# A second level of Strassen for two of the seven products of seven SwiGLU pairs

## The chip, the cores and the metric

The kernel runs on one core of a Trainium2 chip. The metric is the device time of one execution in microseconds (us). Three runs of the kernel before took 2426.53, 2428.89 and 2431.48 us; their median, 2428.89 us, is the time before.

## The reference, cut to what matters

One layer of a hybrid decoder for a prompt of 1024 tokens and eight single sample tokens that use the same weights. Three token mixers (a gated convolution, a state-space scan, attention into a memory) are merged by `w_merge_o`; then comes the part that is changed:

```python
xp = xp + swiglu(rmsnorm(xp, norm_ffn_w[l]), w_ffn_gate[l], w_ffn_up[l], w_ffn_down[l])
...
y_prompt = rmsnorm(xp, norm_final_w)
```

The same is done for the samples. In words: with x the normalized activations (1024 features), h = silu(x·Wgate) * (x·Wup), and the output adds h·Wdown. FFN_HIDDEN is 2816, so Wgate and Wup are 1024 x 2816 and Wdown is 2816 x 1024. All is fp32.

## The kernel before, in words

**Layout.** Prompt and samples stand side by side as the 1032 columns (TT) of feature-major tiles of 128 partitions; half of them is HT = 516. A hidden block is 128 of the 2816 hidden features (22 blocks). A fp32 matrix product is done as three fp32r matmuls, hi·hi, hi·lo and lo·hi: every weight tile and every activation tile exists as `hi` (a copy in fp32r, on ScalarE) and `lo` (what the copy lost, a subtraction on VectorE). This pair of operations is called a split here: `st_split` (L251, its copy L254 and subtraction L255) for weights of 512 or 1024 columns, `split_to` (L392, L393 and L395) for activations.

**One level of Strassen.** Gate, up and most of down are done in pairs of hidden blocks (for down: pairs of output blocks) by `strassen` (L318). The activations are cut in four quadrants, features 0 to 511 and 512 to 1023 by columns 0 to 515 and 516 to 1031; the weights of the two blocks in four as well. Instead of eight quadrant products there are seven, each of a sum of weight quadrants with a sum of activation quadrants. The seven sums of activations are called forms, B11, T1, nT2, B21, T3, B22 and T4; they are made once (`form`, `last_forms`) and stay in SBUF as hi and lo tiles, six in the pool "acts" and T4 in the pool "fx". The sums of weights are made anew for every pair on VectorE: L293 and L294 in `st_sums`, L299 and L300 in `st_adds2`, all of 512 columns. `st_raw` loads the weights of a block. A product (`st_prod`, the matmul is L267) is 4 blocks of 128 features x 3 hi/lo combinations x 2 column pieces (256 and 260) = 24 matmuls, collected in a PSUM tile of 516 columns. PSUM tiles m0, m1 and m2 are used in turn; T3 is added to the tile that already holds nT2 (and B11), after VectorE or ScalarE have read it, T4 to the same one after T3. In an early chain L372 is VectorE's read of nT2, for which T3 waits, and L381 its read of T3, for which T4 waits.

**The pairs.** The loop at L1978 runs over eleven pairs of hidden blocks: (0,9), (1,5), (2,6), (3,7), (4,8), (11,15), (12,16), (13,17), (14,18), (10,19), (20,21). For each, `hidden_pair` (L1950) does a chain of products for gate (names g0, g1, ...) and one for up (u0, u1, ...; the number is that of the pair's first block). The first four pairs are called early: products B11 and B21 of their first block were made ahead by `st_early` (L271) and stored, so their chains have five products. The other seven pairs, numbered 4 to 10, have seven products for gate and seven for up. Behind gate and up follow silu, the product of both, four sums that make the forms of the down projection, and their stores to DRAM (`hf_d`; for the last pairs and (0,9) the plain blocks go to `h_d`).

**Down.** Two parts. In each, first the product of a single hidden block (or two) with its rows of Wdown, 16 groups of 6 (or 12) matmuls called pd (L2078, read from PSUM at L2083 to L2085); beside them the forms of the part are loaded and split (`hidden_forms`), and the weights of the first down pair are prepared (`st_begin`, L306). Then come four chains of seven products, `d00` to `d06` in part 0 and `d10` to `d16` in part 1 (in the trace with an m behind the name: d00m).

**What sets the order.** The engines run their queues in program order, and a scheduler in the framework orders the instructions by its own estimate of their durations when the program is built; `in_turn` fixes the order of loads and of splits among themselves, `tc.issue_after` puts an instruction behind another, and `tick` runs one piece of deferred work from the list `pend` at a marked place. Nearly all DMAs are issued by SyncE's one queue (SP), in order. GpSimd has work only in the scan, around 1000 to 1300 us of the span (L1040 scales the states, L1089 decays them). In that stage L168 and L178 are splits of weights and of activations, L1031 masks a product of 128 columns that it reads from PSUM, and L1059 multiplies 512 columns that it reads from PSUM.

Pools that are touched: "weights" with three raw, three hi and three lo tiles of 1024 columns, "acts" with 12 hi and 12 lo tiles, "ev" with five, "fx" with two, PSUM "sm" with two tiles.

Of the kernel before, what the change touches and what calls it, by code (L numbers as in the profile page):

```python
# [9 lines left out]
F32 = mybir.dt.float32  # L10
# [7 lines left out]
P = 128  # L18
D = 1024
T = 1024  # L20
# [23 lines left out]
def tile_kernel(ctx: ExitStack, tc, a, o):  # L44
# [9 lines left out]
    cp = ctx.enter_context(tc.tile_pool(name="const", bufs=1))  # L54
    wp = ctx.enter_context(tc.tile_pool(name="weights", bufs=3))
# [34 lines left out]
    tri = cp.tile([P, P], F32, tag="tri", name="tri")  # L90
# [140 lines left out]
    count = [0]  # L231

# [3 lines left out]
    HALF = ((0, 256), (256, HT))  # L236

# [50 lines left out]

    def st_sums(src1, src2, nm, sums, behind=None):
        raw1, raw2 = st_raw(src1, f"{nm}r1"), st_raw(src2, f"{nm}r2")  # L290
        sa = sums(f"{nm}sa")
        with nullcontext() if behind is None else tc.issue_after(behind):
            V.tensor_add(sa[:, :512], raw2[:, :512], raw2[:, 512:])  # L293
        V.tensor_add(sa[:, 512:], sa[:, :512], raw1[:, :512])  # L294
        return raw1, raw2, sa, st_split(sa, f"{nm}S")

    def st_adds2(raw1, raw2, sa, nm, sums):
        sb = sums(f"{nm}sb")
        V.tensor_add(sb[:, :512], raw1[:, :512], raw2[:, :512])  # L299
# [17 lines left out]
    def strassen(src1, src2, forms, nm, sums, outs, early=None, after_t3=None, ready=None, hook=None, add=False, begun=None, mid=None):  # L317
# [6 lines left out]
        tags = ("m0", "m1", "m2") if count[0] % 2 == 0 else ("m2", "m1", "m0")  # L324
# [87 lines left out]
    e_d = dram("e_d", [7, P, TT])  # L412
    q_d = dram("q_d", [8, P, TT])
# [8 lines left out]
    tail_sc = cp.tile([P, 1, 10, 8], F32, tag="tail_sc", name="tail_sc")  # L422
    tail_xc = cp.tile([P, 3, 11, 8], F32, tag="tail_xc", name="tail_xc")
    qs = cp.tile([P, 8, NS], F32, tag="qs", name="qs")
# [1135 lines left out]
    if True:  # L1560
# [212 lines left out]
        att_stack.close()  # L1773
        ph2 = ctx.enter_context(tc.tile_pool(name="ph2", bufs=1))
# [73 lines left out]
    def form_second(kt):  # L1848
        form("B21", kt, normed(kt + 4, 0))
# [57 lines left out]
    fx["T4"] = lambda part, nm: pfx.tile([P, 2, HT], F32R, tag=part, name=nm)  # L1907
# [36 lines left out]
    def last_forms():  # L1944
        for kt in range(4):
            t2, b21 = x2[kt][:, HS[0]], x2[kt + 4][:, HS[0]]
            V.scalar_tensor_tensor(t2, t2, -1.0, b21, op0=ALU.mult, op1=ALU.subtract)
            form("T4", kt, t2, freed[0])
# [29 lines left out]
    for n, (j, j2) in enumerate(pairs):  # L1978
# [18 lines left out]
        for f, t in enumerate((b11, t1, t2, b21, t3_, b22, t4)):  # L1997
            SY.dma_start(hf_d[f, n - 1], t)
# [58 lines left out]
    for part, js in enumerate(([0], [9, 10])):  # L2057
# [6 lines left out]
        begun = st_begin(*down_src(part, 0), f"d{part}0", ev_sums)  # L2064
# [3 lines left out]
        for m in range(KD):  # L2068
            if not part:
                x2[m] = big(f"x3_{m}")  # L2070
            for half in range(2):
# [12 lines left out]
                else:  # L2084
                    puts.append(S.copy(t, hv(ps)).ins)  # L2085
        count[0] += 1
# [180 lines left out]
```

## Time and profile before

| | |
|---|---|
| runs of the kernel before | 2426.53, 2428.89, 2431.48 us |
| profiled execution, in all | 2428.33 us |
| its span (first to last instruction) | 2426.6 us |
| mean granted TensorE clock | 0.998 |
| gate and up of pairs 4 to 10 | 1898 to 2178 us of the span |
| first part's pd products | 2178 to 2191 us |
| d00 | 2191 to 2212 us |
| DRAM traffic by DMA | 407.94 MB |

The span is the time between the first and the last instruction that the profiler recorded; the profiled execution's own time has 1.73 us more, which lie before and behind it. PE is the TensorE's matmul, PEld its weight load, DVE VectorE, ACT ScalarE, POOL GpSimd, SP SyncE, whose queue issues DMAs. In a row of the timeline or of the chain of waits the first number is the start in us from the span's beginning, the second the duration, then engine, line, operation, output tile and inputs with their sizes; in brackets stands the idle time before it and what ended it. In the chain, a row with "x120" is a run of so many instructions of one kind. In a row of groups the numbers behind the bar are busy time in all and mean duration in ns, then the idle time before the group's instructions. A row by stretches has start and end, length, and then for each engine the busy time with its count of instructions.

### The profile page before, as it was taken

The numbers are of one execution on the slowest core, as the hardware profiler recorded it, in microseconds if no ns is written. First come the engines' busy times: TensorE is split into PE (matmuls) and PEld (weight loads), VectorE is DVE, ScalarE is ACT, GpSimd is POOL, SyncE is SP. The second block draws the span as 40 slices with busy tenths as digits, with TensorE's granted clock in tenths as the row PEclk, the third lists the DMA queues.
The fourth block names the chain that finished last, engine by engine and source line by source line (L and its number), as shares of the span: only waits on it lengthen the run. The fifth ranks groups of instructions, "written<-read, shape, count | busy, mean of one in ns | idle before, by whom it ended". The sixth has DMA issues, their size and how long they took to land. (4 is left out here: it accounts for less than half of the span.)

```text
span 2426.6 us, 45180 instructions
## 1 busy us (share of the span) xinstructions
PE 2397.0 (99%) x18716; PEld 2279.9 (94%) x18716; DVE 1613.8 (67%) x2597; ACT 1091.9 (45%) x1740; POOL 106.9 (4%) x163
## 2 busy tenths in 40 slices
PE   8999999999999999999999999999999999999998
PEld 6999999999999999888888887899999999999998
DVE  6844677777777675568687773454777655567965
ACT  6643555455453543656555542223543333343423
POOL 0000000000000000212212000000000000000000
PEclk9999999999999999999999999999999999999999
DMA  6444423444354345768887797864455333354622
GB/s 203 136 150 164 135 84 114 140 140 131 112 158 118 106 126 179 225 223 272 257 283 215 252 337 234 276 213 150 148 178 168 101 104 103 94 178 154 192 88 79
DMA packets 357716, 407.94 MB, mean 168 GB/s; under 512 B 16270, under 2 KB 277502, under 8 KB 357503
## 3 DMA queue, kind: packets, MB, share of 16 engines
q1 hardware_dynamic: 334374, 341.79, 45.2%
q10 hardware_dynamic: 23137, 63.26, 6.8%
q8 instruction: 147, 2.41, 0.4%
q14 instruction: 58, 0.48, 0.1%
HBM read 288.85 MB, written 116.38 MB: 167 GB/s over the span
## 5 line engine op out<-in xcount | busy, mean ns | idle before, releaser
L1007 ACT ACTIVATE r<-r,acum 128x128 f32<-128x128 f32 x256 | 79.3, 391 | 3.5 <-DMA r<-ac_d 2.6
L796 DVE SCALAR_TENSOR_TENSOR ax<-u,prm,ax 128x1024 f32<-128x1024 f32 x44 | 56.4, 1282 | 0.0
L948 ACT ACTIVATE st<-st,es 128x128 f32<-128x128 f32 x128 | 41.3, 392 | 19.1 <-DMA st<-in_state_ssm_dram 14.5
L1040 POOL TENSOR_TENSOR xdd<-xdt,decst 128x512 f32<-128x512 f32 x32 | 34.3, 1072 | 284.2 <-DVE xdt L1036 278.4
L1034 DVE TENSOR_TENSOR r<-r,cbm 128x1024 f32<-128x1024 f32 x32 | 39.2, 1224 | 4.3 <-ACT r L1009 2.4
L950 DVE SCALAR_TENSOR_TENSOR st<-sr,dts,st 128x128 f32<-128x128 f32 x128 | 41.0, 355 | 0.4
L1059 DVE TENSOR_TENSOR y<-po,ea 128x512 f32<-128x512 f32 x28 | 19.3, 690 | 31.3 <-PE po L1055 31.3
L1076 PE MATMUL pss<-xdd,bT 128*128 128x512 f32 x64 | 34.5, 620 | 3.7 <-ACT bT L1033 3.1
L954 DVE SCALAR_TENSOR_TENSOR sr<-st,sr 128x128 f32<-128x128 f32 x128 | 36.1, 292 | 1.1
L1497 DVE TENSOR_TENSOR yr<-po,yr 128x1032 f32<-128x1032 f32 x8 | 9.8, 1230 | 39.5 <-PE po L218 39.5
L1063 PE MATMUL py<-r,xdt 128*64 128x128 f32 x512 | 35.0, 279 | 0.0
L1009 ACT ACTIVATE r<-r 128x1024 f32<-128x1024 f32 x32 | 33.9, 1058 | 0.7
L1089 POOL TENSOR_TENSOR s<-s,cdec 128x512 f32<-128x512 f32 x28 | 33.1, 1181 | 1.8 <-DVE s L1082 1.5
L1883 DVE TENSOR_TENSOR x<-pm,xT 128x516 f32<-128x516 f32 x15 | 10.4, 694 | 32.3 <-PE pm L1869 32.3
L1800 DVE TENSOR_TENSOR gt<-po,gt 128x1032 f32<-128x1032 f32 x8 | 9.9, 1232 | 32.4 <-PE po L218 31.1
L1063 PEld LDWEIGHTS py<-r,xdt 128*64 128x64 f32 x512 | 27.3, 136 | 4.4 <-issue 1.0
L1055 PE MATMUL po<-bc,s 128*128 128x128 f32 x224 | 29.6, 275 | 0.0
L1055 PEld LDWEIGHTS po<-bc,s 128*128 128x128 f32 x224 | 28.0, 191 | 1.0
L1612 ACT ACTIVATE pr<-psa,mx 128x256 f32<-128x256 f32 x32 | 14.9, 470 | 30.1 <-DVE mx L1610 30.1
L799 DVE SCALAR_TENSOR_TENSOR ax<-u,prm,ax 128x1032 f32<-128x1032 f32 x22 | 28.4, 1290 | 0.0
L1600 DVE SCALAR_TENSOR_TENSOR kc<-kc,qb 128x256 f32<-128x256 f32 x64 | 23.9, 423 | 6.3 <-DMA qb<-qs_d 6.3
L793 ACT ACTIVATE ax<-u,prm 128x1024 f32<-128x1024 f32 x22 | 27.4, 1246 | 1.2 <-ACT u L875 0.4
(9245 smaller groups left out, 8948.9 us busy)
## 6 DMA issues: line engine op xcount, KB each, us to landing
r<-ac_d SPq DMA_DIRECT2D x32, 512.0 KB
gt_d<-G ACTq DMA_DIRECT2D x24, 516.0 KB
gt<-gt_d SPq DMA_DIRECT2D x24, 516.0 KB
xs_d<-ax ACTq DMA_DIRECT2D x22, 516.0 KB
zs<-zs_d SPq DMA_DIRECT2D x16, 516.0 KB
yb_d<-x SPq DMA_DIRECT2D x16, 516.0 KB
in<-yb_d SPq DMA_DIRECT2D x16, 516.0 KB
st<-in_state_ssm_dram SPq DMA_DIRECT2D x32, 256.0 KB
```

What stands on the lines that cost most here:

```text
L796: V.scalar_tensor_tensor(acc[:, :T], u[:, j : j + T], w[j], acc[:, :T], op0=ALU.mult, op1=ALU.add)
L948: S.activation(st[:, i], st[:, i], AF.Copy, scale=es[:, g * 4 + i, b : b + 1])
L950: V.scalar_tensor_tensor(st[:, i], rb, dts[:, g * 4 + i, b : b + 1], st[:, i], op0=ALU.mult, op1=ALU.add)
L954: V.scalar_tensor_tensor(rb, st[:, i], 1.0, rc, op0=ALU.mult, op1=ALU.mult, accum_out=ys[:, g * 4 + i, b : b + 1],)
L1007: S.activation(r[:, j, :], r[:, j, :], AF.Relu, scale=-1.0, bias=acum[:, c, h : h + 1])
L1009: S.activation(r, r, AF.Exp, scale=-1.0)
L1034: V.tensor_tensor(r, r, bc(cbm.unsqueeze(1), [P, HPG, P]), op=ALU.mult)
L1040: G.tensor_tensor(b3(xdd, HPG), b3(xdt, HPG), bc(decst[:, c, hs].unsqueeze(2), [P, HPG, 64]), op=ALU.mult)
L1055: PE.matmul(po[:, t * P : (t + 1) * P], state["s"][:, t * P : (t + 1) * P], bcg[1][:, cs], start=True, stop=True,)
L1063: PE.matmul(py[hp : hp + 64, (h // 2) * P : (h // 2 + 1) * P], xdt[:, h * 64 : (h + 1) * 64], r[:, (h % 2) * 4 + h // 2, :], start=True, s ...
L1076: PE.matmul(pss, bT, xdd, start=True, stop=True)
L1089: G.tensor_tensor(b3(s_new, HPG), b3(state["s"], HPG), bc(cdec[:, c, hs].unsqueeze(2), [P, HPG, 64]), op=ALU.mult,)
```

## The change

The seven pairs 4 to 10 no longer do B21 and T4 as two of the seven products. In their chains (`chain`, new) five products are left: B11, T1, nT2, T3, B22. B21 and T4 of gate and up, which use the same form for both, are taken together as a 2 x 2 block problem (two weight halves of 256 features, gate and up, against two column halves of 258) and done by a second level of Strassen: `leaf`, seven products of 6 matmuls of 258 columns each. l = 0 is the leaf of B21, l = 1 that of T4.

- **Order.** The two leaves of pair n run inside the chains of pair n+1, one in gate's and one in up's: after B11 the leaf's products 0 and 1, after T1 2 and 3, after nT2 4 and 5, after T3 product 6. The chains of pair 4 have no leaf beside them; the leaves of pair 10 run between the 16 pd products of part 0, and `st_begin` of the first down pair is moved behind the eighth of these. Silu and the product of gate and up of a pair are finished when its leaves are (`first_done`, `second_done`), one pair later.
- **Reads of PSUM.** Each chain has three reads of 516 columns on VectorE and four on ScalarE; each leaf eight of 258 columns, all on VectorE, that add to or subtract from the chain's outputs.
- **Leaf forms.** Seven sums of quarter quadrants for each leaf. `leaf_forms` builds them from the raw forms B21 and T4, which `form_second` and `last_forms` now also store to `lr_d` (eight DMAs). It runs in pieces through `pend` during pairs 1 to 3: eight sums (L2004 on of the new kernel) and fourteen splits. Two forms of each leaf stay in SBUF, in the tiles that B21 had; five of each are stored to `lf_d` and loaded again for every pair into a ring of four tiles (`ring_load`), ten loads per pair, each issued behind the product that frees a tile.
- **Leaf weights.** `leaf_begin` loads 2 x 2 and 4 blocks of 128 x 128 and makes four sums of 256 columns; `w_half` splits them. Chains, too, now split halves of 512 columns with `w_half`, eight splits of 512 and one of 256 per chain and leaf.
- **GpSimd.** All sums of weights go through `plus`. It is VectorE for pair 0, GpSimd from pair 1 on, and VectorE again in the pd stage: three sums of 512 per early chain, four of 512 and four of 256 per later chain with its leaf.
- **Room.** Some constants of the earlier stages (tri, tail_sc, tail_xc, qs) move to a pool that is closed before the FFN; T4 uses tiles of the ring.

```diff
+    adder = [V]
+    def plus(out, x, y):
+        return adder[0].tensor_tensor(out, x, y, op=ALU.add)
     def st_sums(src1, src2, nm, sums, behind=None):
...
-            V.tensor_add(sa[:, :512], raw2[:, :512], raw2[:, 512:])
-        V.tensor_add(sa[:, 512:], sa[:, :512], raw1[:, :512])
+            plus(sa[:, :512], raw2[:, :512], raw2[:, 512:])
+        plus(sa[:, 512:], sa[:, :512], raw1[:, :512])
...
-        V.tensor_add(sb[:, :512], raw1[:, :512], raw2[:, :512])
+        plus(sb[:, :512], raw1[:, :512], raw2[:, :512])
...
+    def leaf_prod(po, w, at, l, i, start):
+        t = ring.popleft() if i < 5 else leaf_tiles[l, i]
+        for k in range(2):
+            ks = slice(at + k * P, at + (k + 1) * P)
+            for n, (wt, x) in enumerate(((w[0], t[:, k, :]), (w[0], t[:, 2 + k, :]), (w[1], t[:, k, :]))):
+                PE.matmul(
+                    po, wt[:, ks], x, start=(start and k == 0 and n == 0), stop=(k == 1 and n == 2),
+                    skip_group_check=True,
+                )
+        if i < 5:
+            ring_load()
...
+    def leaf(l, n, tiles, og, ou, after):
...
+        w = w_half(t1[:, :512], f"{nm}w1")
+        leaf_prod(pa, w, 0, l, 0, True)
+        add(g1, pa)
+        pb = fresh(1)
+        leaf_prod(pb, w, 256, l, 1, True)
+        add(u2, pb)
+        sub(g2, pb)
+        yield
...
+    def chain(i, src1, src2, nm, o):
...
+        w = w_half(raw1[:, :512], f"{nm}A")
+        sa = ev_sums(f"{nm}sa")
+        plus(sa[:, :512], raw2[:, :512], raw2[:, 512:])
+        plus(sa[:, 512:], sa[:, :512], raw1[:, :512])
+        plus(raw1[:, :512], raw1[:, :512], raw2[:, :512])
+        plus(raw1[:, 512:], raw1[:, 512:], sa[:, 512:])
...
+        w = w_half(sa[:, 512:], f"{nm}S2")
+        st_prod(forms, pa, w, 0, "nT2", False)
+        V.tensor_tensor(o12, hv(pa), o22, op=ALU.subtract)
+        yield
+        w = w_half(raw1[:, :512], f"{nm}T")
+        st_prod(forms, pa, w, 0, "T3", False)
...
+    for n, (j, j2) in enumerate(pairs[:4]):
+        if n == 1:
+            adder[0] = G
+            pend.extend(leaf_forms(0) + leaf_forms(1))
...
+    for n in range(4, len(pairs)):
...
+            side = leaf_next() if n > 4 else iter(())
+            for step, _ in enumerate(
+                chain(2 * (n - 4) + i, *(wblock(ffn[nm], x * P) for x in (j, j2)), f"{nm}{j}", oo)
+            ):
+                next(side, None)
+                if step == 2 and (n > 4 or i):
+                    ready.append(leaf_begin(0, n) if i else leaf_begin(1, n - 1))
...
-        begun = st_begin(*down_src(part, 0), f"d{part}0", ev_sums)
+        if part:
+            begun = st_begin(*down_src(part, 0), f"d{part}0", ev_sums)
...
+                if not part and m < 4:
+                    if half == 0 and m % 2 == 0:
+                        side = leaf_next()
+                    next(side, None)
+                    if m == 0 and half == 0:
+                        ready.append(leaf_begin(1, len(pairs) - 1))
+                        adder[0] = V
+                    if m == 3 and half == 1:
+                        begun = st_begin(*down_src(part, 0), f"d{part}0", ev_sums)
```

194 lines of the change are left out of this document (185 added, 9 removed).

## The prediction

> **What bounds the kernel now.** First the page's head, for the share of each engine, then the table of stretches, to see whether that share holds in the stages that the change touches.
>
> ```profile
> span 2426.6 us, 45180 instructions
> ...
> PE 2397.0 (99%) x18716; PEld 2279.9 (94%) x18716; DVE 1613.8 (67%) x2597; ACT 1091.9 (45%) x1740; POOL 106.9 (4%) x163
> ```
>
> ```profile
> 1798.00:1898.00 100.00, 100.00 (x833) 99.64 (x833) 75.26 (x104) 33.53 (x44) 0.00 (x0) 1.00 0.50 157
> 1898.00:2178.00 280.00, 280.00 (x2359) 280.00 (x2358) 161.37 (x206) 98.13 (x127) 0.00 (x0) 1.00 0.36 113
> 2178.00:2212.00 34.00, 33.29 (x269) 32.18 (x268) 24.34 (x29) 20.30 (x28) 0.00 (x0) 1.00 0.63 200
> ```
>
> The columns are length, then busy time of PE, PEld, DVE, ACT and POOL, the granted clock, DMA share and GB/s. From 1898 to 2178 us, where pairs 4 to 10 of gate and up run, PE is busy all of the time at full clock, DVE 58% of it, GpSimd (POOL) never, the DMA engines 36%. So this stage is bound by TensorE alone, and a matmul left out there is time won, as long as nothing else becomes late. Third, the chain that ended last, for the price of a product:
>
> ```profile
> 1840.83 14.46 PE g2m L267 x120
> ...
> 1898.61 19.96 PE g4m L267 x168
> ```
>
> A full pair member (g4) is 168 matmuls in 19.96 us: 118.8 ns each, 2.85 us for a product of 24. An early one (g2) is 120 in 14.46; at 118.8 ns they would be 14.26, so it already loses 0.2.
>
> **The change part by part.**
>
> *Matmuls.* In seven pairs two of the seven products, of gate and up (48 matmuls together), become seven of six matmuls: 42, each 258 columns wide where the old ones alternate 256 and 260, the same mean. At 118.8 ns that is 4.99 us for 5.70. There are 14 such groups: 14 x 6 x 0.1188 = **9.98 us less** on PE, and a chain (five products and one group) lasts 14.26 + 4.99 = 19.25 us. This is all that can be gained; the rest is what may be given back.
>
> *Vector work in the steady part.* Lengths come from these rows: DVE operations of two SBUF inputs of 512, of PSUM and 516, of PSUM and 128.
>
> ```profile
> 1846.59 0.70 DVE L372 TENSOR_TENSOR g2o<-g2m,g2o 128x516 f32<-128x516 f32 x1 [0.33 <-PE g2m L267]
> 1847.20 0.68 DVE L293 TENSOR_TENSOR u2sa<-u2r 128x512 f32<-128x512 f32 x1
> 1847.80 0.69 DVE L299 TENSOR_TENSOR u2sb<-u2r,u2r 128x512 f32<-128x512 f32 x1
> ```
>
> ```profile
> L1031 DVE TENSOR_TENSOR cbm<-bp,tri 128x128 f32<-128x128 f32 x31 | 8.8, 284 | 14.0 <-PE bp L1026 14.0
> ```
>
> A queue of them starts one each 0.60 us, though each lasts 0.69. Between 128 columns (0.28) and 516 (0.70) I estimate 0.43 for 258, or 0.35 from start to start. Per chain DVE now has 8 splits of 512 and one of 256 (5.1 us), 3 PSUM reads of 516 (1.8), 8 of 258 (2.8), and some 2.4 of products and forms at the end: 12.1 us of 19.25, 63%, hardly more than the 58% before. ACT gets about 7 of 19.25. Neither is a bound by its sum.
>
> *The one tight wait.* On PE the third product of a chain (nT2) is followed by leaf products 5 and 6 (12 matmuls, 1.43 us) and then by T3, which adds to the PSUM tile that DVE must have read first (0.70, and some 0.3 of signalling both ways: in the first row above DVE idled 0.33 until PE's end). So 0.43 us are to spare, if DVE is free when nT2 ends. Behind T3 everything on PE is queued. All other waits of the leaf (its PSUM tile, its splits) have a whole product of 2.85 us as cover.
>
> *Sums on GpSimd.* Four adds of 512 and four of 256 per chain go to a queue that stood empty. Their price, and what they do to DVE, is shown in the earlier stage where GpSimd works; first DVE, then POOL:
>
> ```profile
> 1121.57 1.69 DVE L168 TENSOR_TENSOR wo01l<-wo01r,wo01h 128x1024 fp32r<-128x1024 f32 x1
> 1123.18 0.68 DVE L1059 TENSOR_TENSOR y<-po,ea 128x512 f32<-128x512 f32 x1
> 1123.78 1.47 DVE L178 TENSOR_TENSOR b02l<-in,b02h 128x1032 fp32r<-128x1032 f32 x1
> ```
>
> ```profile
> 1121.13 1.04 POOL L1040 TENSOR_TENSOR xdd<-xdt,decst 128x512 f32<-128x512 f32 x1 [5.37 <-DVE xdt L1036]
> 1122.14 2.03 POOL L1089 TENSOR_TENSOR s<-s,cdec 128x512 f32<-128x512 f32 x1
> ```
>
> A GpSimd operation of 512 takes 1.04 us. The DVE split that began during the first one took 1.69, not the 1.22 that such a split takes alone: it ended 1.09 after GpSimd did. The second GpSimd operation took 2.03: it waited for that split. The DVE operation that reads PSUM (0.68) ran beside it unhurt. So a DVE operation with both inputs in SBUF and a GpSimd add shut each other out for their whole length, and every split can be held by up to 1.04 us. The Trainium skill ("SBUF — State Buffer", section "Who interferes with whom") says the same as a rule: a DVE instruction with two SBUF inputs contends with a GpSimd instruction that reads SBUF, and whoever comes second waits for the whole instruction. By that rule these sums aren't free for DVE; these rows agree with it.
>
> GpSimd needs 4 x 1.04 + 4 x about 0.52 (half, an estimate) = 6.2 us per chain. With no overlap at all, 12.1 + 6.2 = 18.3 of 19.25: DVE still keeps up, but late by one or two adds at times. Ahead of the tight wait stands the split of the next chain's first weights, which can start some 2.5 us before nT2 ends; one add in front of it does no harm, two in a row and the split leave DVE late by some tenths. Bounds per chain: nothing, and one add in front with no spare, 1.04. I take 0.1, by the row where DVE's PSUM read was unhurt: 13 chains, **+1.3** (0 to 13.5).
>
> *Pairs 1 to 3.* GpSimd takes three sums of each member (1.8 us off DVE), and 22 operations for the leaf's forms (14 splits, 8 sums of 516) come to DVE, 2.2 us per member. Where up of one pair ends and gate of the next begins, DVE had no room:
>
> ```profile
> 1836.98 0.69 DVE L381 TENSOR_TENSOR u1o<-u1o,u1m 128x516 f32<-128x516 f32 x1
> ...
> 1845.58 0.68 DVE L255 TENSOR_TENSOR g2Dl<-g2r,g2Dh 128x512 fp32r<-128x512 f32 x1
> ```
>
> From 1836.98 to 1846.59 it idles 0.33 us. In the new order of DVE's queue three leaf operations stand before the L381 subtraction, for which T4 waits, and one leaf operation and a moved sum (u2sb) before the L372 add, for which T3 waits. Laid end to end at 0.60, with the two GpSimd adds that fall there, L381 ends 0.7 us after T4 could have started and L372 0.25 after T3. That is 0.95 at u1 to g2 and again at u2 to g3; at u3 to g4 a B11 product now stands between. **+1.9** (0 to 6 x 1.04 = 6.2).
>
> *The last leaves and d00.* Two leaves now run between the 16 products of pd.
>
> ```profile
> 2177.83:2190.89 13.06, 12.38 (x100) 11.80 (x100) 6.00 (x7) 10.23 (x16) 0.00 (x0) 1.00 0.70 225
> 2190.89:2211.70 20.81, 20.78 (x171) 20.25 (x170) 18.51 (x22) 9.87 (x13) 0.00 (x0) 1.00 0.58 183
> ```
>
> Before, pd takes 13.06 us for 96 matmuls (11.4). After, PE has 11.4 + 9.98 = 21.4 there, and DVE's queue up to the S split of d00 holds 33 operations of together 21 us: three form splits of 1.23, five leaf splits and two shorter ones, the leaf's reads, the splits and sums of d00. They run neck and neck; following their order I get 1.8 us of waits where 1.66 were. Then d00 needs its T weights after B11, B21 and nT2 (some 11.4 us), and DVE still has eight form splits (9.8 us), four reads and three sums ahead of that split: T comes 2.1 us late, where the whole of d00 lost 0.85 before (20.81 for 168 x 0.1188 = 19.96). Together 0.2 + 1.3 = **+1.5** (0 to 6).
>
> *DMA.* Sizes per issue, and a stage that moved much:
>
> ```profile
> g11r<-in_w_ffn_gate_dram SPq DMA_DIRECT2D x2, 512.0 KB
> ...
> hf_d<-u11o SPq DMA_DIRECT2D x4, 258.0 KB
> ```
>
> ```profile
> 1500.00:1600.00 100.00, 98.57 (x653) 85.05 (x653) 46.42 (x41) 22.54 (x26) 0.00 (x0) 1.00 0.87 302
> ```
>
> Per pair of 38.5 us: ten forms of 516 KB, four weights and twice 512 KB of leaf weights, seven stores of 258: 9.9 MB (of 1024 KB), 270 GB/s, so 0.78 to 0.86 of the DMA engines by the two rows (0.87 for 302, 0.36 for 113). A form is loaded four uses ahead; the shortest lead, from the end of the leaf's first product to its fifth, is 7.8 us, against 1.7 of transfer at 302 GB/s. All issues stand in SP's one queue; ahead of that load wait two to four stores of finished pairs, for DVE. I take **0** (0 to 1 us in each of 13 chains). The eight stores of raw forms ahead of the FFN, and the moved constants, change nothing that PE waits for.
>
> *Sum.* The profiled execution took 2428.33 us in all (span 2426.6). 2428.33 - 9.98 + 1.3 + 1.9 + 1.5 = 2423.05. The median of the three runs is 0.56 above that execution; in its terms **2423.6 us**, 0.22% below 2428.89. About 0.2% (4.9 us) is what a measurement of this kernel tells from no change.
>
> **The rivals.**
>
> *All hidden* (2418.9 in the same terms): DVE's 63% and the long covers speak for it, the dense stretch at 1837 to 1847 us against it.
>
> *Lock at the tight wait* (slower): GpSimd's adds fall ahead of the read before T3. With one add of 1.04 and no room for the split, T3 is 0.61 late; with two, 1.65; the mean, 1.13, over 13 chains is 14.7, and the six early members and d00 take 3.8 and 1.5: 2428.89 - 9.98 + 14.7 + 5.3 = 2438.9. It decides from 0.4 us a chain on (13 x 0.4 = 5.2, which eats the forecast's gain). For it: the locked rows. Against it: DVE isn't short of time by its sum.
>
> *Forms late*: the DMA engines at up to 0.86 share and one queue in order. One microsecond at the fifth leaf product in 13 chains: 2423.6 - 1.3 + 13 = 2435.3. Against it: 302 GB/s were moved with PE at 98.57%.
>
> *No saving*: a matmul that changes weights each time and reads a form with a gap between rows costs more than 118.8 ns; from 48/42, 136 ns, nothing is saved, and 2428.89 + 4.7 = 2433.6. Every matmul of before has its own weight load (PE and PEld both x18716), which speaks against it.
>
> **How the numbers follow.** Forecast 0.47 (its own range 2420 to 2427, of which about 0.32 lies below 2424.0), all hidden 0.17, lock 0.20, forms late 0.10, no saving 0.06. Faster by over 0.2%: 0.32 + 0.17 = 0.49; within: 0.15 of the forecast, and 0.08 of mild lock or late forms, 0.23; slower: 0.28. The range reaches from all hidden to the middle of the lock and late cases: 2418 to 2436.
>
> **What would show it.** The leaf's line with some 588 matmuls near 119 ns and a chain of 19.25 us; PE's idle time before T3, the dense stretch with PE idle by about a microsecond at T4 and T3 of u1, g2, u2, g3; splits of 512 that last up to 1.7 us wherever GpSimd adds; d00 near 22 us. Wrong if PE idles at leaf products until a DMA of the forms lands, if DVE's busy share in the steady part passes 85%, or if T3's wait recurs in every chain.

## The result and the profile after

The changed kernel took **2451.65 us** (median of four runs, 2450.34 to 2454.40) where the kernel before took 2428.88 beside it: ratio 1.0095, 95% interval 1.0077 to 1.0112. It is slower by about 23 us; 2423.6 were predicted, and the range ended at 2436. The profiled execution took 2450.34 us with a span of 2448.6, 22.0 us above that of before.

The head of the page answers to that of before: PE has the same busy time with 84 matmuls fewer, and it is idle longer.

```profile
span 2448.6 us, 45899 instructions
...
PE 2397.8 (98%) x18632; PEld 2277.8 (93%) x18632; DVE 1682.3 (69%) x2727; ACT 1118.8 (46%) x1824; POOL 266.6 (11%) x293
```

Where the time went is read from a table by stages, cut at the starts of PE's groups: g0 (pairs 0 to 3), g4 (pairs 4 to 10), the first pd product, d04, the end. Columns as in the prediction; first before, then after.

```profile
1783.01:1898.45 115.44, 115.44 (x962) 115.03 (x961) 85.50 (x119) 41.06 (x53) 0.00 (x0) 1.00 0.50 157
1898.45:2177.89 279.44, 279.44 (x2354) 279.44 (x2353) 160.81 (x205) 98.03 (x126) 0.00 (x0) 1.00 0.36 113
2177.89:2231.47 53.58, 52.87 (x434) 51.76 (x433) 38.70 (x47) 23.72 (x32) 0.00 (x0) 1.00 0.57 182
2231.47:2426.60 195.13, 187.97 (x1506) 185.66 (x1504) 133.77 (x197) 65.23 (x95) 0.00 (x0) 0.99 0.37 120
```

```profile
1782.57:1918.34 135.77, 122.44 (x962) 120.45 (x961) 92.91 (x121) 49.80 (x72) 34.30 (x23) 0.95 0.61 194
1918.34:2183.83 265.49, 262.28 (x2186) 261.66 (x2185) 206.13 (x304) 110.46 (x184) 123.83 (x104) 0.99 0.89 261
2183.83:2252.96 69.13, 64.35 (x518) 62.17 (x517) 55.63 (x76) 30.64 (x42) 3.19 (x4) 1.00 0.72 230
2252.96:2448.60 195.64, 188.26 (x1506) 185.87 (x1504) 133.56 (x197) 65.25 (x95) 0.00 (x0) 0.99 0.37 120
```

| stage | work of PE at 118.8 ns, after | loss against it or before | predicted |
|---|---|---|---|
| pairs 0 to 3 | as before | 135.77 - 115.44 = **+20.3** | +1.9 |
| pairs 4 to 10 | 14 x 14.26 + 12 x 4.99 = 259.5 | 265.49 - 259.5 = **+6.0** | +1.3 |
| pd, d00, d02 | 53.58 + 9.98 = 63.56 | 69.13 - 63.56 = **+5.6** | +1.5 |
| rest and start | as before | +0.1 | 0 |

Together 32.0, less the 9.98 of matmuls left out: 22.0. The largest part is in pairs 0 to 3, where PE has exactly the matmuls of before. It is idle 13.33 us there (135.77 - 122.44), and the same 962 matmuls are busy 7.00 us longer (122.44 - 115.44).

The list of waits of PE in that stage (what waited for whom, us in total, times, longest) names single waits, not one that recurs. Its first three:

```profile
PE u2m L271 <- DVE u2o L390: 4.1, 1, 4.1
PE g2m L271 <- DVE g2o L381: 3.1, 1, 3.1
PE u0m L271 <- DVE u0o L381: 3.0, 1, 3.0
```

In the changed kernel the last sum of weights is L309 (L300 before), the read of nT2 L381 (L372) and the read of T3 L390 (L381). The third of these waits (u0's T3 for VectorE's read of nT2), in the timelines of PE, VectorE and GpSimd:

```profile
1806.95 0.51 PE L271 MATMUL u0m<-T30h,u0Th 128*128 128x256 f32 x2 [2.97 <-DVE u0o L381]
```

```profile
1798.85 0.68 DVE L259 TENSOR_TENSOR u0Dl<-u0r,u0Dh 128x512 fp32r<-128x512 f32 x1
1802.09 1.78 DVE L309 SCALAR_TENSOR_TENSOR g1sb<-g1sa,g1r 128x512 f32<-128x512 f32 x1 [2.56 <-POOL g1sa L296]
1803.79 0.68 DVE L2019 TENSOR_TENSOR lf<-lr,lf 128x516 fp32r<-128x516 f32 x1
...
1806.21 0.68 DVE L381 TENSOR_TENSOR u0o<-u0m,u0o 128x516 f32<-128x516 f32 x1
```

```profile
1798.92 1.77 POOL L296 TENSOR_TENSOR g1sa<-g1r 128x512 f32<-128x512 f32 x1 [488.96 <-DMA g1r<-in_w_ffn_gate_dram]
1800.77 1.29 POOL L296 TENSOR_TENSOR g1sa<-g1sa,g1r 128x512 f32<-128x512 f32 x1
1802.01 1.30 POOL L296 TENSOR_TENSOR g1sb<-g1r,g1r 128x512 f32<-128x512 f32 x1
```

L309 is the fourth sum of weights, of the *next* chain (g1), and it stayed on VectorE. It stands in VectorE's queue ahead of the read of u0's nT2, and it needs g1's second sum, which is GpSimd's now, which waited for g1's weights. So VectorE stood idle for 2.56 us, took 1.78 for the sum beside GpSimd's third, did the leaf's forms and a subtraction (L380) that follow, and only then the read. In the kernel before the same sum stood behind that read, with no wait:

```profile
1803.27 0.70 DVE L372 TENSOR_TENSOR u0o<-u0m,u0o 128x516 f32<-128x516 f32 x1 [1.32 <-PE u0m L267]
...
1805.81 0.69 DVE L300 SCALAR_TENSOR_TENSOR g1sb<-g1sa,g1r 128x512 f32<-128x512 f32 x1
```

So the change didn't only move the sum's inputs: in the order that the scheduler then chose, the sum also moved ahead of the read. A wait behind L309 is found at u2 as well: GpSimd's first sum waits 8.23 us for u3's weights, L309 waits 5.11 for GpSimd, and L390 behind it gates T4. The list of waits of VectorE in the stage has that line for five of the six chains whose sums moved:

```profile
DVE u3sb L309 <- POOL u3sa L296: 5.1, 1, 5.1
...
DVE g1sb L309 <- POOL g1sa L296: 2.6, 1, 2.6
DVE g2sb L309 <- POOL g2sa L296: 2.4, 1, 2.4
DVE g3sb L309 <- POOL g3sa L296: 2.4, 1, 2.4
...
DVE u2sb L309 <- POOL u2sa L296: 1.8, 1, 1.8
```

The steady part is as predicted. Eight chains with their leaves, from g12 to u10:

```profile
1987.03:2141.31 154.28, 154.28 (x1298) 154.28 (x1297) 123.65 (x189) 63.68 (x108) 77.03 (x64) 1.00 0.90 268
```

That is 19.29 us a chain where 19.25 are work, though VectorE is busy 80% of the time. The 6.0 us of this stage are elsewhere: 1.6 in pair 4, and 4.0 in the last chain, u20, whose T3 stood 2.15 us because a split of the down projection's forms, itself idle 3.14 us for its load and ScalarE, was ahead of the read:

```profile
2176.02 0.51 PE L271 MATMUL u20c<-T30h,u20T 128*128 128x256 f32 x2 [2.15 <-DVE u20o L2155]
```

```profile
2174.13 1.23 DVE L404 TENSOR_TENSOR B1102al<-B,B1102ah 128x1032 fp32r<-128x1032 f32 x1 [3.14 <-ACT B1102ah L402]
2175.28 0.69 DVE L2155 TENSOR_TENSOR u20o<-u20c,u20o 128x516 f32<-128x516 f32 x1
```

Each of the four longest waits was paid a second time: the matmuls behind it ran at a lower granted clock. The last value but two of a row is the clock; here are the stretches of the product behind the waits of 2.97, 2.15 and 4.15 us (behind that of 3.12 it is as behind 2.97):

```profile
1806.95:1811.60 4.65, 4.65 (x26) 4.65 (x27) 1.07 (x1) 0.62 (x1) 1.98 (x2) 0.63 0.40 116
2176.02:2180.66 4.64, 4.64 (x26) 4.64 (x27) 3.58 (x5) 1.69 (x2) 0.00 (x0) 0.63 0.99 354
1884.12:1889.60 5.48, 5.48 (x25) 5.48 (x26) 4.64 (x6) 1.91 (x3) 0.00 (x0) 0.50 0.85 287
```

At full clock such a stretch takes 3.10 us, so 1.5 us came on top of three of the waits and 2.4 on top of the longest. The length of a wait alone doesn't decide this. Two of the kernels below show it: the first row stands behind a wait of 1.62 us (d00, with only the leaf's sums on GpSimd), the second behind one of 3.17 us (g2, with VectorE's last sum behind the read of T3).

```profile
2205.82:2210.47 4.65, 4.65 (x23) 4.45 (x24) 4.65 (x8) 1.42 (x2) 0.00 (x0) 0.63 0.41 124
```

```profile
1858.42:1861.52 3.10, 3.10 (x26) 3.10 (x27) 1.68 (x2) 0.24 (x1) 0.00 (x0) 1.00 0.84 293
```

The Trainium skill ("TensorE: Matmul & The Clock Gate", section "Part 1: The HAM clock gate (the "warmup" mystery)") states that the clock falls to half after an idle window of about 3.4 us of a free-running count. Here waits of 1.62 and 2.15 us were enough and one of 3.17 was not, so 3.4 us is not the least wait in this kernel. That equal waits end differently would fit a count that doesn't start with the wait; no run here shows the count.

### The profile page after: what moved, and what is told of

The parts are those of the page before. It is cut to its first block, busy times and chain, and to the rows that moved or that the text cites. A ratio compares the mean times of both kernels' runs of the same rounds, so it can differ in the third digit from the quotient of the medians.

```text
span 2448.6 us, 45899 instructions
## 1 busy us (share of the span) xinstructions
PE 2397.8 (98%) x18632; PEld 2277.8 (93%) x18632; DVE 1682.3 (69%) x2727; ACT 1118.8 (46%) x1824; POOL 266.6 (11%) x293
## 5 line engine op out<-in xcount | busy, mean ns | idle before, releaser
L1623 ACT ACTIVATE pr<-psa,mx 128x256 f32<-128x256 f32 x32 | 14.9, 470 | 30.2 <-DVE mx L1621 30.2
```

## The experiments

Each time stands beside runs of the kernel before on the same chip (medians 2427.9 to 2429.6); "stage" is the length from g0 to g4 in the profiled execution, 115.44 us before. The first kernel and five others below have the same instructions in pairs 0 to 3; their stage took 117.26 to 119.73 us, so a difference of 2.5 us between two stages can be chance.

**Which part of the change costs in pairs 0 to 3.** Theory A: the sums on GpSimd. Rival B: the leaf's forms. First the sums back on VectorE, then the sums alone on GpSimd in the kernel before.

```diff
     for n, (j, j2) in enumerate(pairs[:4]):
         if n == 1:
-            adder[0] = G
...
+    adder[0] = G
     for n in range(4, len(pairs)):
```

> The changed kernel, with the sums of weights of pairs 1 to 3 back on VectorE (GpSimd only from pair 4 on). In the changed kernel pairs 0 to 3 lost 20.3 us against the kernel before. Theory A: the sums on GpSimd cause it, since the last sum of the next chain (L309, still on VectorE) stands in VectorE's queue ahead of reads of PSUM and waits there for GpSimd. Then at most 4 us are lost in pairs 0 to 3 and the time is 2432 to 2438 us. Rival B: the leaf's forms (22 operations on VectorE, their loads and stores in SP's queue ahead of weights) cause it: at least 14 us stay, 2445 us or more.

Measured 2433.07 us, ratio 1.0016 (1.0006 to 1.0025); the stage 118.11, +2.7.

```diff
     for n, (j, j2) in enumerate(pairs):
+        adder[0] = G if 1 <= n < 4 else V
...
-            V.tensor_add(sa[:, :512], raw2[:, :512], raw2[:, 512:])
+            plus(sa[:, :512], raw2[:, :512], raw2[:, 512:])
```

> The kernel before, with nothing but the three sums of weights of each chain of pairs 1 to 3 moved to GpSimd; no leaf, no leaf forms. Theory A: 12 to 20 us slower than before, 2441 to 2449 us, with the waits at the reads of nT2 and T3. Rival B: at most 3 us slower, 2432 us or less.

Measured 2445.43 us, ratio 1.0062 (1.0047 to 1.0077); the stage 128.12, +12.7. So A holds as to the sums: three of them per chain on GpSimd cost 12.7 us without a leaf or a form, the forms cost 2.7 without those sums, and both together 20.3, 4.9 more than one by one. In the second kernel the last sum waits for GpSimd in all six chains, 2.4 to 5.9 us, and the three longest waits of PE (3.3, 2.4 and 1.6 us, at u2, g1 and u0) are for reads of nT2 or T3.

**Is GpSimd of use in pairs 4 to 10?** No sum on GpSimd, then the leaf's sums alone.

```diff
-            adder[0] = G
             pend.extend(leaf_forms(0) + leaf_forms(1))
```

> The changed kernel with no sum on GpSimd at all. Pairs 0 to 3 as in the first kernel of this call. In pairs 4 to 10 VectorE then has 12.1 + 4 x 0.60 + 4 x 0.35 = 15.9 us of work per chain of 19.25. If that fits, the time is within 3 us of the first kernel, 2430 to 2438 us; if GpSimd is needed there, a chain grows by 0.5 us or more, 13 chains by 6 or more, 2440 us or more.

Measured 2449.06 us, ratio 1.0096 (1.0058 to 1.0133). Pairs 4 to 10 take 281.51 us, 18 more than with the early sums on VectorE (263.41), so GpSimd is of use. Why is seen in VectorE's queue:

```profile
2009.47 0.42 DVE L296 TENSOR_TENSOR l16a<-l16b 128x256 f32<-128x256 f32 x1 [1.43 <-DMA l16b<-in_w_ffn_up_dram]
...
2011.42 0.69 DVE L2155 TENSOR_TENSOR u12o<-u12c,u12o 128x516 f32<-128x516 f32 x1
```

A leaf sum waits for its weights' DMA, with four more sums behind it, ahead of the read that T3 waits for.

```diff
     def leaf_begin(l, n):
-        plus(t1[:, 256:512], t2[:, 512:768], t2[:, 768:])
+        G.tensor_tensor(t1[:, 256:512], t2[:, 512:768], t2[:, 768:], op=ALU.add)
...
-    adder[0] = G
     for n in range(4, len(pairs)):
```

> The changed kernel with the early sums and the sums of pairs 4 to 10's chains on VectorE, and only the leaf's sums of 256 columns on GpSimd. With no sum on GpSimd (2449 us) the first leaf sum waited 1.4 us at its place in VectorE's queue for its weights' DMA, ahead of the read that T3 waits for. Theory D: without that wait VectorE's 12.1 + 2.4 = 14.5 us of 19.25 fit, 2431 to 2436 us. If the amount of work on VectorE is what costs (four sums of 512 stay there), 2441 us or more.

Measured 2433.91 us, ratio 1.0027 (1.0017 to 1.0036); pairs 4 to 10 take 264.45. With the sums of 512 columns on VectorE and only those of 256 on GpSimd nearly all of the 18 us are back. So four sums of 512 columns a chain on VectorE don't cost them; the leaf's four sums do. Whether by the wait for their load or by their own 1.4 us ahead of the read, this edit doesn't tell, since it takes both away.

**GpSimd's adds themselves.** One of the three moved sums, which VectorE's last sum doesn't read; then three adds on GpSimd that nobody reads.

```diff
-        V.tensor_add(sb[:, :512], raw1[:, :512], raw2[:, :512])
+        plus(sb[:, :512], raw1[:, :512], raw2[:, :512])
```

> The kernel before, with only one of the sums of each chain of pairs 1 to 3 on GpSimd: the one of 512 columns that no operation left on VectorE reads (L299, the first half of the sums for T3). VectorE's last sum then waits for nothing on GpSimd. Theory D: what costs is that an operation on VectorE waits, at its place in the queue, for a chain weights' DMA, GpSimd, VectorE. Here that wait is not there: at most 3 us slower than before, 2429 to 2432 us, though GpSimd's operations and VectorE's splits still shut each other out. If that exclusion, or GpSimd's length, is what costs: 5 us or more slower, 2434 us or more.

Measured 2429.85 us, ratio 1.0004 (0.9994 to 1.0013): the same as before.

```diff
     def st_adds2(raw1, raw2, sa, nm, sums):
+        for _ in range(3):
+            G.tensor_tensor(idle[0], sa[:, :512], sa[:, 512:], op=ALU.add)
```

> The kernel before, its own sums on VectorE, with three more adds of 512 columns on GpSimd in each chain of pairs 1 to 3 whose results nothing reads. If GpSimd's adds cost by shutting out VectorE's splits (up to 1.04 us each), pairs 0 to 3 lose 5 us or more: 2433 us or more. If that exclusion is hidden and the moved sums cost by their place in chains of waits: within 2 us of before, 2426 to 2430 us.

Measured 2432.91 us, ratio 1.0020 (1.0011 to 1.0030). The stages of the two, first with one sum, then with the idle adds:

```profile
1780.52:1896.90 116.38, 115.58 (x962) 114.73 (x961) 85.99 (x113) 40.62 (x53) 10.24 (x6) 1.00 0.51 156
```

```profile
1780.97:1900.27 119.30, 117.03 (x962) 115.12 (x961) 90.74 (x119) 40.91 (x53) 32.21 (x18) 1.00 0.49 152
```

+0.9 and +3.9. Neither theory had the 3.9: GpSimd's presence costs something (each idle add lasts 32.21 / 18 = 1.79 us, and VectorE is busy 5 us longer than before), about a third of what the moved sums cost. The profiled execution with the idle adds, 2430.48 us, was the fastest of ten; by the medians the adds cost 5.0 us, and the three moved sums 15.9.

**The place of VectorE's last sum.** Two kernels with L309 behind a read, in the changed kernel: of its own chain's nT2, and of T3 of the chain before.

```diff
+                with tc.issue_after(freed[0]):
+                    st_last(raw1, sa, sb)
             wT = st_split(sb, f"{nm}T")
```

> The changed kernel, sums on GpSimd as in it, but in the early chains the last sum of weights (the one left on VectorE) comes behind that chain's own read of nT2, so it no longer stands ahead of the reads of the chain before it. Theory A: the waits of u0's T3 (2.97 us) and u2's T4 (4.15 us) go, and with them the slow matmuls behind them; 8 to 14 us are won back, 2438 to 2444 us. Rival B, or the sums themselves being late: T3 then waits for its weights instead, and the time stays at 2448 us or more.

Measured 2468.37 us, ratio 1.0161 (1.0146 to 1.0176), the slowest of all. The reads are no longer held, but T3 waits for its weights in every chain, the longest:

```profile
PE g1m L271 <- ACT g1Th L258: 4.2, 1, 4.2
PE g2m L271 <- ACT g2Th L258: 4.2, 1, 4.2
```

The edit put sum, copy and split of T3's weights in a row behind the last read before T3, so it says little on A.

```diff
+        with nullcontext() if read_t3[0] is None else tc.issue_after(read_t3[0]):
             V.scalar_tensor_tensor(
                 sb[:, 512:], sa[:, 512:], -1.0, raw1[:, 512:], op0=ALU.mult, op1=ALU.subtract
             )
```

> The changed kernel, sums on GpSimd as in it, but in the early chains the last sum of weights (L309, on VectorE) is placed behind the read of T3 of the chain before it: behind both of that chain's reads that TensorE waits for, and ahead of its own chain's read of nT2. Theory A with the place in the queue as the cause: the loss of 20.3 us in pairs 0 to 3 falls to 8 us or less, 2435 to 2440 us. If instead the sums are late whatever the place, T1 or T3 waits for its weights and the time is 2448 us or more, as with the last sum placed later still (2468 us).

Measured 2446.41 us, ratio 1.0072 (1.0056 to 1.0088); the stage 133.12, +17.7. A miss for A: PE still waits for reads of nT2 (g2 3.2, g3 3.1, u0 2.4, g1 2.3 us). But nothing on VectorE waits for GpSimd in this stage any more. Ahead of each of these four reads VectorE has operations beside GpSimd's three sums, which take 1.5 to 1.8 us where such an operation takes 0.69 otherwise. The last ones ahead of g3's read, and then GpSimd's sums:

```profile
1883.60 1.78 DVE L2219 TENSOR_TENSOR u2o<-u2o,g2o 128x516 f32<-128x516 f32 x1
1885.31 1.79 DVE L259 TENSOR_TENSOR g3Dl<-g3r,g3Dh 128x512 fp32r<-128x512 f32 x1
1887.02 1.76 DVE L2221 SCALAR_TENSOR_TENSOR u2o<-u2o,g2o 128x516 f32<-128x516 f32 x1
```

```profile
1884.79 1.76 POOL L296 TENSOR_TENSOR u3sb<-u3r,u3r 128x512 f32<-128x512 f32 x1
1886.51 1.71 POOL L296 TENSOR_TENSOR u3sa<-u3sa,u3r 128x512 f32<-128x512 f32 x1
```

So here it is the exclusion of VectorE and GpSimd, which the prediction had as a rival for another place, that makes the reads late: the wait for GpSimd is gone and the loss stays. In the changed kernel it has a part too. Its 121 operations of VectorE are busy 92.91 us in this stage (102.29 here); the kernel with the early sums on VectorE has 18 more and 97.39, so that I estimate 85 us for the 121 alone (97.39 - 18 x 0.69).

**All four sums on GpSimd** in pairs 1 to 3, so that no sum on VectorE waits for it; in the kernel before and in the changed one.

```diff
-        V.scalar_tensor_tensor(
-            sb[:, 512:], sa[:, 512:], -1.0, raw1[:, 512:], op0=ALU.mult, op1=ALU.subtract
-        )
+        plus(sb[:, 512:], sa[:, 512:], raw1[:, 512:])
```

> The kernel before, with all four sums of weights of each chain of pairs 1 to 3 on GpSimd, the last one too (added with the other sign, the products' signs changed to match). With three of them there it took 2445.4 us. Theory D: no sum on VectorE waits for GpSimd any more, so most of the 12.7 us in pairs 0 to 3 come back: 2429 to 2435 us, though GpSimd has one operation more. Rival E: the way from the weights' DMA over GpSimd to the splits is too long for the three buffers of weights, wherever VectorE waits: 2442 us or more.

Measured 2447.13 us, ratio 1.0078 (1.0063 to 1.0093); the stage 134.46, +19.0.

> The changed kernel with all four sums on GpSimd in the early chains too. Theory D: of the 20.3 us lost in pairs 0 to 3 at most 7 stay (the forms' part is 2.7): 2433 to 2439 us. Rival E: 2447 us or more.

Measured 2460.70 us, ratio 1.0132 (1.0117 to 1.0147); the stage 145.31, +29.9. By their times both are as rival E had put it. VectorE had no such wait any more, but ScalarE got one, in the first of the two kernels at u1:

```profile
1833.93 0.62 ACT L378 COPY u1o<-u1o 128x516 f32<-128x516 f32 x1 [11.73 <-DMA u1o<-e_d]
```

This copy of an early product stood 11.73 us for its load, and the splits behind it with it. The load stood in SP's queue behind weights that waited for one of three buffers, which the late sums gave back late.

**More room for weights**, meant to free the loads from the sums: with three sums on GpSimd (before, changed), then with four.

```diff
-        raw1, raw2 = st_raw(src1, f"{nm}r1"), st_raw(src2, f"{nm}r2")
+        raw1 = sums(f"{nm}r1")
+        in_turn("raw", SY.dma_start(raw1.rearrange("p (k c) -> p k c", k=KD), src1))
+        raw2 = st_raw(src2, f"{nm}r2")
```

> The kernel before with three sums of weights on GpSimd in pairs 1 to 3 (2445.4 us), and in these chains the first block's weights are loaded to a tile of the pool of five that also holds the sums, so that a load no longer waits for a buffer that the chain before frees with its last sum. Theory E: the three weight buffers and SP's queue in order tie the next loads to the late sums; without that tie at most 5 of the 12.7 us stay: 2428 to 2434 us. If GpSimd's length itself is too late for the splits: 2441 us or more.

Measured 2439.06 us, ratio 1.0043 (1.0028 to 1.0058); the stage 126.52, +11.1 where 5 were expected at most.

> The changed kernel with the same: the first block's weights of pairs 1 to 3 in a tile of the pool of the sums. That pool also holds the leaf's raw forms here. Theory E: of the 20.3 us lost in pairs 0 to 3 at most 10 stay: 2436 to 2442 us. Otherwise 2448 us or more.

Measured 2447.86 us, ratio 1.0078 (1.0057 to 1.0099); the stage 132.58, +17.1. That is 1.6 and 3.2 us less than without the room, little beside the 2.5 that can be chance. The loads weren't freed: in the first of the two SP's queue waits 4.1 to 9.7 us for VectorE's last sums in four chains, since the pool's five tiles come free with the sums as well. There the last sum of g2 (L310) again stands ahead of g1's read of nT2:

```profile
1819.48 1.73 DVE L310 SCALAR_TENSOR_TENSOR g2sb<-g2sa,g2r 128x512 f32<-128x512 f32 x1 [3.18 <-POOL g2sa L292]
1821.14 0.68 DVE L381 TENSOR_TENSOR g1o<-g1o,g1o 128x516 f32<-128x516 f32 x1
```

> The kernel before with both: all four sums of pairs 1 to 3 on GpSimd, so that no sum on VectorE waits for it, and the first block's weights in a tile of the sums' pool, so that the loads (and the early products behind them in SP's queue, for which ScalarE waited 11.7 us) are not tied to the sums. Each alone left 11.1 us or more in pairs 0 to 3. Theory F, both ties together cost what the idle adds don't: at most 6 us stay (the idle adds lost 3.9), 2430 to 2435 us. If GpSimd's own length is too late for the splits: 2438 us or more.

Measured 2439.46 us, ratio 1.0045 (1.0028 to 1.0062); the stage 129.02, +13.6. By the time a miss, but PE's waits in the stage are these two and 0.9 us at u1:

```profile
PE g2m L267 <- DVE g2o L385: 6.5, 1, 6.5
PE g2m L267 <- ACT g2o L348: 3.3, 1, 3.3
```

```profile
ACT g2o L383 <- DMA g2o<-e_d: 14.9, 1, 14.9
```

With all four sums on GpSimd g1, u2, g3 and u3 have no wait at all. Nearly all of the loss is one chain, g2, where ScalarE stood 14.9 us for the load of one early product. SP's queue shows why that load was late:

```profile
SPq L299 <- POOL u2sb L292: 7.9, 1, 7.9
```

The load was issued at 1838.98 us (at 1828.19 in the kernel before), behind g3's weights at 1837.31, which had waited for a tile until u2's last sum on GpSimd ended at 1837.28. So here, too, the loads were tied to the sums. GpSimd took 6.0 us for u2's four sums, from 1831.24 on; four on VectorE are 2.4. By its time and by this chain of waits the kernel leaves GpSimd's length as a possible cause.

> The changed kernel with both. Theory F: of the 20.3 us in pairs 0 to 3 at most 9 stay (3.9 as with the idle adds, 2.7 of the forms, and some for both together), 2436 to 2441 us. Otherwise 2446 us or more.

Measured 2454.72 us, ratio 1.0112 (1.0096 to 1.0127); the stage 140.79, +25.4: a miss, with waits at g2, u2 and g3 of 2.9 to 4.9 us.

**The end of the pairs and pd.** The forms of part 0 behind u20's read; then one leaf in pd in place of two; then the leaf's forms spread thinner; then no leaf in pd.

```diff
-        hidden_forms(part, fs, NAMES[:3])
+        with nullcontext() if part else tc.issue_after(read_nt2[0]):
+            hidden_forms(part, fs, NAMES[:3])
```

> As the kernel with the early sums on VectorE (2433.1 us), and the loads and splits of the down projection's first forms put behind u20's read of nT2 on VectorE. That read stood behind a form split that waited for a DMA, and T3 waited 1.9 us for it. If the place is the cause, the wait goes: 2430 to 2432 us. If the forms then come late for d00, the loss only moves: 2433 to 2437 us.

Measured 2433.88 us, ratio 1.0029 (1.0016 to 1.0042). First the kernel with the early sums on VectorE, pairs 4 to 10 and then pd to d04, then this one:

```profile
1901.79:2165.20 263.41, 261.07 (x2187) 260.23 (x2186) 204.62 (x304) 110.43 (x184) 126.76 (x104) 1.00 0.88 263
2165.20:2234.13 68.93, 64.91 (x519) 62.40 (x518) 55.91 (x77) 30.65 (x42) 3.18 (x4) 1.00 0.73 233
```

```profile
1902.52:2163.47 260.95, 260.47 (x2186) 260.05 (x2185) 205.36 (x302) 109.32 (x183) 125.05 (x104) 1.00 0.88 264
2163.47:2236.65 73.18, 64.78 (x518) 62.33 (x517) 57.50 (x79) 32.14 (x43) 3.22 (x4) 1.00 0.69 226
```

2.46 us are won in the stage that ends with u20 and 4.25 lost from pd to d04: the place was the cause of that wait, and in the new place the work costs more.

```diff
-        jobs.append((0, n, s1[:, HS[0]], u1[:, HS[0]], lambda done=done: first_done(*done)))
+        first_done(*done)
...
+            if i:
+                jobs.append((0, n, tiles[0][:, HS[0]], oo[0][:, HS[0]], lambda: None))
```

> As the kernel with the forms behind the read, and the first leaf of each pair runs in the same pair's chain of up, so that one leaf instead of two is left for the pd stage. If VectorE's queue in pd is what costs there (26.0 us where 21.4 are work), about half of that is won: 2427 to 2430 us. If the loss is the stage's whatever stands in it (loads of forms, d00's weights): 2430 to 2433 us.

Measured 2439.50 us, ratio 1.0052 (1.0034 to 1.0069): slower. From pd to d04, 65.09 us are 6.5 above the work of 58.6, no better than with two leaves. Pairs 4 to 10 took 272.81, 8.3 above their work of 264.5 (13 groups of leaf products now), where the kernel with the early sums on VectorE lost 3.9; the second leaf of a pair, now in the next pair's chain of gate, waits there 0.5 to 0.7 us for VectorE's reads in five pairs.

```diff
-            pend.extend(leaf_forms(0) + leaf_forms(1))
+            for k, f in enumerate(leaf_forms(0) + later[:3]):
+                pend.extend([f, None] if k % 2 else [f])
```

> As the kernel with one leaf in pd, and the leaf's forms spread thinner: eleven of sixteen pieces over pairs 1 to 3, five in the first chain of pair 4. The kernel with the early sums on VectorE lost 2.7 us in pairs 0 to 3 to these pieces. If they are the cause, at most 1 us is left there and the time is 1 to 2.5 us below that of the kernel with one leaf in pd, 2425 to 2429 us; if not, it is the same as that within 0.5 us.

Measured 2437.87 us, ratio 1.0046 (1.0031 to 1.0061); the stage 118.79, where the kernel with one leaf in pd had 119.73. The median is 1.6 us below that kernel's, inside what was expected of the forms, but its five runs lie between 2433.99 and 2444.74, and the stage still loses 3.4 us against before. That spreading wins the forms' 2.7 us back is not shown.

```diff
                     if half == 0 and m % 2 == 0:
-                        side = leaf_next()
-                    next(side, None)
+                        jobs.popleft()[4]()
```

> The kernel with the early sums on VectorE (2433.1 us), with the two leaves of pair 10 left out (its B21 and T4 products are missing from the output). They are 9.98 us of TensorE's work. If they are also what makes pd and d00 lose 5.4 us more than before, the time is 2433.1 - 10.0 - 5.4 = 2417 to 2419 us; if the stage loses that anyway, by the moved preparation of d00, 2422 to 2424 us.

Measured 2415.35 us, ratio 0.9943 (0.9926 to 0.9960), a little below the lower expectation. From pd to d04:

```profile
2164.28:2218.70 54.42, 53.04 (x435) 51.90 (x433) 41.24 (x49) 23.52 (x32) 0.00 (x0) 1.00 0.60 195
```

0.8 us above before instead of 5.4: most of the loss in pd comes with the two leaves, beyond the 9.98 us of their matmuls.

None of these kernels that does the whole work is faster than the one before. The best of the changed ones, with the early sums on VectorE, is 0.16% slower.

## Why the prediction was wrong

**Matmuls, 9.98 us less: right.** The leaf's line has 588 matmuls, and a chain with its leaf lasts 19.29 us.

**Steady part, 0.1 us a chain: right** where it was meant, 0.04 in the eight chains shown; also that T3 has enough to spare and that the DMA engines (0.90 at 268 GB/s) keep PE waiting nowhere there. The work under it was put too low: VectorE was busy 15.5 us a chain (123.65 / 8) and not 12.1, GpSimd 9.6 (77.03 / 8) and not 6.2, so part of this is luck. (A pair's loads and stores add up to 9.8 MB, not 9.9, and 12 chains have a leaf, not 13; neither matters.) The stage lost 6.0 and not 1.3, at its two ends. In pair 4 no leaf stands between nT2 and T3, so that u4's T3 waited 0.93 us for the read; the prediction had no term for this pair. The prediction saw the splits of forms that come at u20 only as work of the pd stage; it didn't look at what VectorE's queue holds during u20, the last chain.

**Pairs 1 to 3, "+1.9 (0 to 6 x 1.04 = 6.2)": the step that failed.** The prediction took GpSimd's sums as 1.8 us taken off VectorE and laid VectorE's operations end to end at 0.60, with two GpSimd adds as the only hindrance. It had one such sum (u2sb) ahead of a read that T3 needs, but priced it at its length and gave it no wait. In the trace that sum waits 1.8 to 5.1 us in five of six chains, since its inputs now come from a weights' DMA over GpSimd, and what stands behind it in the queue are reads that PE needs. The bound of 6.2 was a bound of the exclusion only, and took one add per chain: the idle adds put that at 3.9 us by the profile and 5.0 by the medians, but three sums beside three operations of VectorE made reads late by up to 3.2 us at one T3. A bound of the wait would have had to come from the loads, which land when three buffers and one queue in order let them. With 20.3 in place of 1.9 the sum would give 2442; the rest of the miss is in the two terms beside it, 6.0 for 1.3 and 5.6 for 1.5.

**The lock as a rival** (2438.9) had a loss on the right scale, but put it at T3 in every later chain, and by exclusion. There GpSimd did the opposite of harm: with the sums on VectorE the same chains lose 18 us. Why the same move is good in one stage and bad in the other is not shown. In pairs 4 to 10 all sums are GpSimd's, so that no sum on VectorE waits for one; but with all four sums on GpSimd in pairs 1 to 3 the stage lost 19.0 and 29.9, more than with three. Another difference is that pairs 1 to 3 load early products, for which ScalarE stood in those kernels.

**pd and d00, +1.5: too small**, 5.6. With the early sums on VectorE it was 5.4, and 0.8 without the last leaves, so 4.5 of it are theirs. Part of it is a wait that the prediction didn't have: the second leaf stands 1.3 us for ScalarE's copy of weights that GpSimd summed late, since their load landed only then (GpSimd's first sum for it begins at 2192.89, 3.1 us before that leaf's first product).

**Clock.** The prediction priced a wait at its length. Behind the long ones the next product took 1.5 to 2.4 us more; in pairs 0 to 3 three such products make 5.5 of the 7.0 us by which the same matmuls were busy longer.

**What is shown and what not.** Shown: the sums on GpSimd cause most of the loss in pairs 0 to 3; taken back, 2.7 of the 20.3 us stay, and moved alone they cost 12.7. Adds on GpSimd that nobody waits for cost about a third of that. In the changed kernel and in the kernel before with three sums moved, the traces show a way: VectorE's last sum waits for GpSimd ahead of reads that PE needs. Not shown: that this way is the whole cause, since no edit that took it away made the stage as quick as before. With the last sum behind the read of T3, VectorE's operations were slow beside GpSimd's; with all four sums on GpSimd, loads came late and ScalarE stood for them. GpSimd's length is in both, and no kernel separates it; how the 20.3 us divide among the three stays open. Each edit also changed the order that the scheduler chose for the rest. An order written by hand for these chains wasn't tried, nor a fourth buffer of weights beside the three.

## What to carry to other kernels

When work is moved to another engine, look for what stays behind and reads its result: that instruction inherits the waits of the new engine, and in a queue in order it passes them on to all that stands behind it. Look also at whether it still stands where it stood, since the scheduler may order the queue anew, and at what VectorE has to do beside the helper's operations. To move the reader as well is not enough by itself: here the loads and the copies behind them inherited the wait. Price an added wait by when its input can arrive, DMA and buffers included, and leave room for a lower clock behind it, which cost 1.5 to 2.4 us more for each of the four longest waits here.

## What the runs showed of the hardware

- An add of 512 columns on GpSimd took 1.26 to 1.30 us at its quickest in pairs 1 to 3, not the 1.04 of the scan's multiplication, and 1.75 to 2.28 beside VectorE's operations with two inputs in SBUF.
- Three such adds per chain with no one waiting cost 3.9 us in six chains. The Trainium skill ("SBUF — State Buffer", section "Who interferes with whom") has the exclusion as a rule; these runs agree that it is there: VectorE's sum of 512 columns took 1.78 us beside a GpSimd add and 0.69 alone. Three operations of VectorE in a row beside three such adds took 1.76 to 1.79 us each.
- The granted clock fell to 0.63 over 4.65 us behind waits of TensorE of 1.62, 2.15 and 2.97 us, and stayed at 1.00 behind one of 3.17 in another kernel.
- The DMA engines worked at 0.90 share and 268 GB/s for 154 us while PE had no idle time.
